# Axial attention: the second score product over all 128 rows, with the keys' low part stacked twice

## The chip, the cores and the metric

The kernel runs as one program on one core of a Trainium2 chip. The metric is the device time of that core in microseconds (us), the median of three runs. TensorE (PE) multiplies, VectorE (DVE), ScalarE (ACT) and GpSimd (POOL) do the elementwise work, and SyncE's queue (SP) issues nearly all transfers.

## The reference

Two layers of a transformer block work on 256 latent tokens and 256 context tokens of width 1024. In each layer three mixers (A: grouped-query attention with axial rotary embedding; B: gated linear attention; C: neighbourhood attention) read one projection of the normalised tokens, are merged under gates and projected out; then a mixture of 32 experts with two experts per token follows. Mixer A, cut to what matters:

```python
q = apply_rope(rms_norm(q_lat.reshape(B, L, 8, 64), q_norm), cos, sin)
k = apply_rope(rms_norm(k_lat.reshape(B, L, 2, 64), k_norm), cos, sin)
k_c = rms_norm(k_ctx.reshape(B, Lc, 2, 64), k_norm)
s = einsum('bqkgd,bskd->bkgqs', q, concat([k_c, k])) * 64 ** -0.5
o = einsum('bkgqs,bskd->bqkgd', softmax(s), v)
```

Eight query heads of 64 columns share two key heads. Latents attend to all 512 tokens. In layer 0 the context attends to its own 256 tokens as well; in layer 1 only the latents are computed on.

## The kernel before, in words

All large products are made in two parts: an operand is split into a high part that TensorE's fast fp32 form (fp32r) holds exactly, and a low rest. A full product is three matmuls, high by high, low by high and high by low (`mm3`, L380 to L382); the low-by-low term is left out. `split` (L291, L292) makes the two parts of the weights on ScalarE and VectorE from pieces of [128, 1024] that stream in (L373).

`attention` (mixer A) first projects keys and values (`projM`). For each of four token tiles `norm_rope` normalises and rotates the keys, and a staging tile `kst` [128 tokens, 2 key heads, 256 columns] is filled: the high part on ScalarE (L852) in columns 0 to 63, a copy of it on GpSimd (L853) in columns 64 to 127, the low part on VectorE (L854) in columns 128 to 191. Columns 192 to 255 are not used. TensorE transposes columns 0 to 127 into `kTs` (L859), so that the high part stands on rows 0 to 63 and again on rows 64 to 127, and columns 128 to 191 into rows 0 to 63 of `kTl` (L860); L861 and L862 copy both out of PSUM. Then the queries are projected, and `prep` makes for each tile `qT`: a head's query with its high part on rows 0 to 63 and its low part on rows 64 to 127 (transposes L880, copy L881).

A score tile of 128 queries is then made by two matmuls into one PSUM bank (`scores`): L888 multiplies all 128 rows of `qT` with `kTs` (high by high plus low by high), L889 multiplies rows 0 to 63 of `qT` with `kTl` (high by low) and adds to it. The page prints the used rows and columns of the array as `128*128` for the first and `64*128` for the second. For the latents these matmuls are 512 columns wide, for the context 256 columns.

`attend` runs over units (pairs of heads) and is one step ahead with the scores: `start` issues the scores of the next step, `finish` then makes the softmax of the step before (row maximum L796 on VectorE, exponential L799 on ScalarE, reciprocal L800 and scaling L802 on VectorE), the transposes of the probabilities (L944 for the latents, L950 for the context), their copies out of PSUM (L945, L951), the products with the values (L958, 64 columns of the array) and their split (L787, L788). A step of the latents issues L888, L889, L888, L889, a step of the context that sequence twice. Layer 0 has 8 steps of latents and 4 of context, layer 1 has 8 of latents.

Scores, transposes and value products share four PSUM banks; projections and merges have four others. The order on every engine is not written by hand: a planner takes the traced program, with priorities that follow the order of tracing, simulates all engines and their waits, and fixes each engine's order ahead of time. It puts matmuls of the merge of mixer B (`br`, `pT`) and of the projections of mixer C (`pM`) between the steps of the attention. Behind the mixers `out_norm` (matmuls `wo`) makes the tokens of the experts. The experts' weights (L1463, L1468) go into the place that the mixers' tiles leave, so those transfers wait for `wo` and later matmuls.

Of the kernel before, what the change touches and what calls it, by code (L numbers as in the profile page):

```python
# [27 lines left out]
# columns of w_in  # L28
A_Q, A_K, B_Q, B_K, B_V, B_R, B_A, C_Q, C_K, C_V, GATE = 0, 512, 768, 1024, 1280, 1792, 2304, 2336, 2848, 3360, 3872

# the order in which the mixers' weights stream in, one [128, 1024] piece each
# [27 lines left out]
# columns of the per-partition biases  # L59
# [9 lines left out]
# sections of the constants  # L69
# [9 lines left out]
# ranks of the experts of layer 0, by load but for experts 0 and 1, whose weights come in early:  # L79
# with 128 slots, with 64, the others with 32; the order of their halves of 128 slots  # L80
# [29 lines left out]
def groups(l):  # L110
    """The experts (in layer 0 by rank of their load) that share 256 slots, in two halves of one, two or four experts"""
    if l:
        return [((4 * d, 4 * d + 1), (4 * d + 2, 4 * d + 3)) for d in range(8)]
    a, b = 2 + NHOT, 2 + NHOT + NMID
    kinds = {"H": [(i,) for i in range(2, a)], "M": [(0, 1)] + [(i, i + 1) for i in range(a, b, 2)],
             "Q": [tuple(range(i, i + 4)) for i in range(b, NE, 4)]}
    halves = [kinds[k].pop(0) for k in HALVES]
    assert not any(kinds.values())
    return list(zip(halves[::2], halves[1::2]))


def _constants():
# [5 lines left out]
    i = np.arange(128)  # L128
# [4 lines left out]
    t = np.arange(256)  # L133
# [4 lines left out]
    cos, sin = np.cos(ang), np.sin(ang)  # L138
# [4 lines left out]
    # slots of the experts by rank  # L143
# [15 lines left out]
    # pairs of tokens of a block of 64 whose highest different bit is the level's  # L159
# [5 lines left out]
def _layout(inp):  # L165
    """The arrays of setup_inputs() as the program reads them."""
    g = {k: np.asarray(v) for k, v in inp.items()}
    f32 = np.float32
    o = {}
# [3 lines left out]
    # w_mod: [layer, group of four 512-column chunks, k tile, half of the group][partition][2 chunks x 512]  # L173
# [10 lines left out]
    # branches in the order in which they are merged: gla, attention, neighbourhood  # L184
# [42 lines left out]
    # the relative bias of every (query, key), outside of the window a constant; context keys have none  # L227
# [12 lines left out]
    # experts: [layer, expert][partition][six pieces of 2048]  # L240
# [9 lines left out]
class _Prog:  # L250
# [3 lines left out]
    # ---- tiles  # L254
# [14 lines left out]
    def rsqrt(self, v, w, tmp=None):  # L269
        """v ** -0.5 by Newton's method"""  # L270
# [18 lines left out]
    def split(self, src, hi, lo, eng=None):  # L289
        """hi + lo = src, exactly, each with 12 significant bits"""  # L290
        self.nc.scalar.copy(hi, src)  # L291
        (eng or self.nc.vector).tensor_tensor(lo, src, hi.bitcast(F32), op=ALU.subtract)  # L292

    def stats(self, x):
        """mean and 1 / sqrt(var + eps) of x [128, 1024]"""
# [9 lines left out]
    def norm0(self, x, xh, total=None):  # L305
        """xh = layer_norm0(x), both [128, 1024]; with the sums of x, ScalarE makes those of its squares"""
# [15 lines left out]
    def stats_all(self, xs, apart=False):  # L322
        """stats of tiles together: columns of means, of 1 / sqrt(var + eps), and of the opposites of their products"""
# [25 lines left out]
    def norm_quick(self, x, out, g, b):  # L349
        """out = layer_norm0(x) * g + b, on VectorE alone, and the sums of its rows; x is overwritten"""  # L350
        STT = self.nc.vector.scalar_tensor_tensor
        mu, r, _ = self.stats(x)
        s = self.small(2)
        STT(x, x, mu, g, op0=ALU.subtract, op1=ALU.mult)
        STT(out, x, r, b, op0=ALU.mult, op1=ALU.add, accum_out=s[:, 0:1])
        return s[:, 0:1]

    def norm(self, x, out, g, b, last=None):
        """layer_norm0(x) * g + b, in two steps"""
# [4 lines left out]
    # ---- streams of weights  # L364
    def raw(self, l):
        """A place for weights as they come in; the first ones of layer 1 can't wait for the tokens that use the others"""
# [17 lines left out]
    def projT(self, l, n, ntok):  # L384
        """[128 columns of w_in, tokens] = w^T h^T"""
# [7 lines left out]
    def projM(self, l, names, kper, width, tiles, sub=None):  # L393
        """[tokens, columns of w_in] for the token tiles, one bank each"""
# [17 lines left out]
    # ---- constants  # L412
# [42 lines left out]
    def open(self, name, side, tags):  # L455
        """A pool that shares its place with the one that follows it on the same side"""
# [7 lines left out]
    def later(self, n=400):  # L464
        """What is traced here gives way to the next n instructions"""
# [4 lines left out]
    # ---- modulation  # L470
    def modulation(self, l, groups, tag="raw", tag2="b2", ps="mod"):
        """[128, 512] of group g: row 32 j + s holds 512-column chunk 4 g + j for the latents (s = 0) and the context (s = 1)"""
# [11 lines left out]
        for g in groups:  # L484
# [19 lines left out]
            # the columns: [partition, scale or shift, stream, k tile]  # L504
# [18 lines left out]
    def mod_row(self, l, q, s, tag="o4"):  # L523
        """A modulation vector on every partition: [128, 1024]"""
# [7 lines left out]
    def norm_T(self, l, xs):  # L532
        """h^T of the mixers: modulated layer_norm0 of the four token tiles, in two parts"""
# [25 lines left out]
    # ---- per-layer vectors  # L559
    def vectors(self, l):  # L560
# [5 lines left out]
        # q and k norms with the rotary tables: [tile][q, k][cos, sin][64]  # L566
# [28 lines left out]
    # ---- branch B: gated linear attention  # L595
    def gla_gates(self, l):
        """log decays [tokens, (pair, direction, 2 x 64)] times 16, in two parts"""
# [14 lines left out]
    def gla_decay(self, pair):  # L612
        """Sums of the log decays (times 16) of each tile of tokens: up to and with a token (forward), up to a token (backward)"""
# [22 lines left out]
    def gla_pair(self, l, pair, T):  # L636
# [22 lines left out]
        # decays from a tile's start or end, of the queries and of the keys, in both directions  # L659
# [15 lines left out]
        # what a tile adds to the states of both directions  # L675
# [17 lines left out]
        # scores of a tile with itself, in blocks of 64: one level of the decay's tree after the other  # L693
# [47 lines left out]
        # the states before each tile  # L741
# [36 lines left out]
    # ---- the branches' outputs, transposed: tile k of branch i, in two parts  # L778
# [11 lines left out]
    # ---- attention  # L790
    def softmax(self, P, s, nh, w, mx=None, scale=1.0):
        """P [128, nh, w] = softmax over the last axis of scale * s"""
# [11 lines left out]
    def split2(self, src, hi, lo):  # L804
        """like split, from PSUM"""
# [3 lines left out]
    def norm_rope(self, l, z, nh, i, t):  # L809
        """rms_norm and rotary embedding of z [128, nh * 64] (i: 0 for q, 1 for k)"""  # L810
# [26 lines left out]
    def attention(self, l, T):  # L837
# [7 lines left out]
        for t in range(4):  # L845
# [8 lines left out]
            nc.vector.tensor_tensor(st[:, :, 128:192], o, hi, op=ALU.subtract)  # L854
            kst.append(st)
        for kv in range(2):
            p0, p1 = self.ps("kTs"), self.ps("kTl")
            for t in range(4):
                nc.tensor.transpose(p0[:, 128 * t:128 * t + 128], kst[t][:, kv, 0:128], self.ident)  # L859
                nc.tensor.transpose(p1[:64, 128 * t:128 * t + 128], kst[t][:, kv, 128:192], self.ident)  # L860
            nc.scalar.copy(kTs[:, kv], p0)  # L861
            nc.vector.tensor_copy(kTl[:64, kv], p1[:64])  # L862
# [21 lines left out]
        def scores(qT, kv, pair):  # L884
            def emit(o, i, ks):
                for h in range(2):
                    q = qT[i][:, 2 * pair + h]
                    mm(o[h], q, kTs[:, kv, ks], start=True, stop=False)  # L888
                    mm(o[h], q[:64], kTl[:64, kv, ks], start=False, stop=True)  # L889
# [12 lines left out]
    def attend(self, units):  # L902
        """softmax(scores) V of pairs of heads, for the latents over all keys or for the context over its own; one step ahead with the scores"""
# [64 lines left out]
        for n, (u, i) in enumerate(steps):  # L968
            o = start(u, i)
            # what the next units need is made before this one's end  # L970
# [52 lines left out]
    # ---- merge of the branches  # L1023
# [28 lines left out]
    def out_norm(self, l, T, src):  # L1052
        """x = layer_norm(alpha x + g1 (y w_out)), h2 = modulated layer_norm0(x)"""
# [64 lines left out]
    def h2_done(self, l, t):  # L1118
        """h2, in two parts"""
# [16 lines left out]
    def logits(self, l, t, h):  # L1136
        """the router's products of token tile t, from its layer_norm0"""
# [24 lines left out]
    def warm(self, n, x, name="warm"):  # L1162
        """Products that nothing reads, from x [128, some columns] on: they keep TensorE's clock up until its next work"""
# [6 lines left out]
    # ---- routing  # L1170
    def top2(self, l, t0, t1, T):
        """The two experts of the tokens of tiles t0 to t1, and their gates"""
        nc, c = self.nc, self.c
        TT, TS, STT, RED = nc.vector.tensor_tensor, nc.vector.tensor_scalar, nc.vector.scalar_tensor_tensor, nc.vector.tensor_reduce
        if t0 == 0:
# [6 lines left out]
            # the second choices' gates in two parts, what the first ones' are more in three  # L1182
# [18 lines left out]
        def mark(oh, x, m, weights, w, op=ALU.is_equal):  # L1201
            """op(1 where the maximum m comes first)"""
# [41 lines left out]
    def route(self, l, T):  # L1244
        """each token's place in its experts' slots"""
# [19 lines left out]
        # how many tokens before this one chose each expert, and how many chose it at all  # L1265
# [6 lines left out]
        if l == 0:  # L1272
            # experts by how many tokens chose them, on the partitions and along the rows
# [21 lines left out]
        # places beyond the slots' end, and below it  # L1295
# [17 lines left out]
        with self.later():  # L1313
            # what does not fit: blocks of 128 slots, expert after expert
# [9 lines left out]
            # from a token's place to its place there; negative where it fits  # L1324
# [7 lines left out]
            # the blocks' experts  # L1332
# [7 lines left out]
    def slot_rows(self, s, T):  # L1340
        """slots of all tokens on every partition, first and second choices"""
# [12 lines left out]
    # ---- experts  # L1354
    def one_hot(self, iota, w, T, d):
        """[tokens, slots]: 1 where the token has the slot, and where it is the first choice's"""
# [7 lines left out]
    def slot_gates(self, p, OH, O1, T):  # L1364
        """p [slots, 5]: the parts of the gates of the slots' tokens"""
# [6 lines left out]
    def gather_T(self, OH, w, T):  # L1372
        """the slots' tokens, transposed: [d, k, slot]"""
# [14 lines left out]
    def spots(self, rows, col, T):  # L1388
        """[slots, tokens]: 1 where the token has the slot"""
# [8 lines left out]
    def expert_tail(self, h1, h3, gate, w2, halves, end=False):  # L1398
        """Y = (silu(h1) * h3 * gate) w2, in two parts; w2(f, n, i): weights of half i"""
# [19 lines left out]
    def combine(self, CY, T, last):  # L1419
        """x += g2 * the experts' outputs"""  # L1420
# [13 lines left out]
    def expert(self, l, u):  # L1434
        """The weights of an expert (in layer 0 of rank u): [128, six pieces, 2048]"""
# [7 lines left out]
    def load(self, l, us, n, js, step=2048, most=99, after=None):  # L1443
        """Pieces js of the weights of the experts us"""
# [3 lines left out]
        for j in js:  # L1448
            for i in range(len(us)):
# [7 lines left out]
                if n < 6 or n >= 6 + extra:  # L1457
                    x = self.t([128, 2048], "pre" if n < 0 else "ew" if n < 6 else "ewb", name="ew")
                    if after is not None:
                        # not before other weights  # L1460
# [10 lines left out]
    def experts(self, l, T):  # L1471
# [51 lines left out]
        # the second products of one pair of experts come after the first ones of the next  # L1523
# [10 lines left out]
    def overflow(self, l, T):  # L1534
        """the tokens beyond an expert's slots, in blocks of 128"""
# [44 lines left out]
    def final_norm(self, l, T, lgb):  # L1580
        """x = layer_norm(alpha x + g2 experts)"""
# [32 lines left out]
    def run(self):  # L1614
# [7 lines left out]
        for l in range(NL):  # L1622
# [42 lines left out]
            if l:  # L1665
                # what the context's tokens leave
# [44 lines left out]
```

## Time and profile before

| what | value |
|---|---|
| time, median of 3 runs | 2171.39 us (2170.97 to 2172.95) |
| profiled execution, span | 2169.8 us |
| median beyond that span | 1.6 us |
| PE busy | 1989.3 us, 92% of the span |
| DVE busy | 968.1 us, 45% |
| ACT busy | 561.9 us, 26% |
| POOL busy | 272.2 us, 13% |
| DMA | 562.41 MB, mean 259 GB/s |

The span is the profiled execution from its first to its last instruction. Busy shares are means over stages with different limits: in the mixers (about 200 to 650 us and 1240 to 1650 us) little is transferred, while in the experts (about 650 to 1207 us and 1647 to 2150 us) the DMA engines are busy nearly all the time. Matmuls overlap in PE's pipeline, so the time that one matmul takes from the stream is the distance of its start to the next start, not its duration.

### The profile page before, as it was taken

The numbers are of one execution on the slowest core, as the hardware profiler recorded it, in microseconds if no ns is written. First come the engines' busy times: TensorE is split into PE (matmuls) and PEld (weight loads), VectorE is DVE, ScalarE is ACT, GpSimd is POOL, SyncE is SP. The second block draws the span as 40 slices with busy tenths as digits, with TensorE's granted clock in tenths as the row PEclk, the third lists the DMA queues.
The fourth block names the chain that finished last, engine by engine and source line by source line (L and its number), as shares of the span: only waits on it lengthen the run. The fifth ranks groups of instructions, "written<-read, shape, count | busy, mean of one in ns | idle before, by whom it ended". The sixth has DMA issues, their size and how long they took to land. (4 is left out here: it accounts for less than half of the span.)

```text
span 2169.8 us, 28061 instructions
## 1 busy us (share of the span) xinstructions
PE 1989.3 (92%) x10749; PEld 1179.2 (54%) x10749; DVE 968.1 (45%) x2236; ACT 561.9 (26%) x992; POOL 272.2 (13%) x260
## 2 busy tenths in 40 slices
PE   5999999999998898989899598999996999999995
PEld 2676766777885353445253165786795433333321
DVE  4676765564388131222022765766648222221213
ACT  3443334343333000000000254444543111010000
POOL 1322100011110010111011222100020000000000
PEclk9999999999999999999999798999997999999998
DMA  7436212223328899999998723632466999999995
GB/s 289 164 121 218 78 59 69 93 83 96 126 79 334 367 420 421 371 385 421 419 369 370 270 85 112 197 118 74 139 207 250 387 421 423 421 423 422 421 422 222
DMA packets 113987, 562.41 MB, mean 259 GB/s; under 512 B 13302, under 2 KB 14838, under 8 KB 72120
## 3 DMA queue, kind: packets, MB, share of 16 engines
q1 hardware_dynamic: 113272, 558.85, 66.9%
q8 instruction: 87, 1.43, 0.3%
q10 hardware_dynamic: 576, 1.70, 0.2%
q14 instruction: 52, 0.43, 0.1%
HBM read 557.36 MB, written 3.15 MB: 258 GB/s over the span
## 5 line engine op out<-in xcount | busy, mean ns | idle before, releaser
L1506 PE MATMUL h<-ew,XT 128*64 128x512 f32 (+2 forms) x2048 | 478.3, 611 | 40.0 <-DMA ew<-in_ew_dram 39.8
L1506 PEld LDWEIGHTS h<-ew,XT 128*64 128x64 f32 (+2 forms) x2048 | 146.6, 135 | 326.3 <-issue 248.8
L1414 PE MATMUL Y<-ew,aT 128*64 128x512 f32 (+2 forms) x1024 | 252.4, 598 | 10.1 <-DMA ew<-in_ew_dram 7.9
L292 DVE TENSOR_TENSOR wlo<-raw,whi 128x1024 fp32r<-128x1024 f32 (+1 forms) x140 | 178.9, 1278 | 139.6 <-ACT whi L291 138.4
L1432 POOL TENSOR_TENSOR x<-x,ct 128x512 f32<-128x512 f32 x82 | 105.0, 1307 | 1003.5 <-DVE ct L1431 879.8
L380 PE MATMUL pT<-hThi,whi 128*128 128x512 f32 (+1 forms) x576 | 202.9, 352 | 1.5 <-ACT whi L291 0.8
L291 ACT CAST whi<-raw 128x1024 fp32r<-128x1024 f32 (+1 forms) x140 | 145.4, 1039 | 226.5 <-PE pT L381 116.2
L382 PE MATMUL pT<-hThi,wlo 128*128 128x512 f32 (+1 forms) x576 | 202.3, 351 | 0.2 <-DVE wlo L292 0.2
L381 PE MATMUL pT<-hTlo,whi 128*128 128x512 f32 (+1 forms) x576 | 202.1, 351 | 0.0
L1403 DVE SCALAR_TENSOR_TENSOR act<-h,s,sl 128x512 f32<-128x512 f32 x30 | 22.5, 751 | 325.4 <-PE h L1506 270.5
L1414 PEld LDWEIGHTS Y<-ew,aT 128*64 128x64 f32 (+2 forms) x1024 | 76.0, 133 | 151.0 <-issue 125.7
L807 DVE TENSOR_TENSOR Yl<-Y,Yh 128x512 fp32r<-128x512 f32 x60 | 41.4, 690 | 257.2 <-ACT Yh L806 254.1
L806 ACT CAST Yh<-Y 128x512 fp32r<-128x512 f32 x60 | 35.2, 587 | 462.5 <-PE Y L1414 462.5
L380 PEld LDWEIGHTS pT<-hThi,whi 128*128 128x128 f32 x576 | 109.5, 190 | 22.4 <-issue 4.1
L382 PEld LDWEIGHTS pT<-hThi,wlo 128*128 128x128 f32 x576 | 109.5, 190 | 16.2 <-issue 2.9
L381 PEld LDWEIGHTS pT<-hTlo,whi 128*128 128x128 f32 x576 | 109.6, 190 | 15.2 <-issue 3.0
L380 PE MATMUL pM<-whi,hThi 128*128 128x512 f32 (+1 forms) x304 | 110.7, 370 | 3.6 <-ACT qTkT L645 1.9
L381 PE MATMUL pM<-wlo,hThi 128*128 128x512 f32 (+1 forms) x304 | 111.8, 369 | 0.0
L382 PE MATMUL pM<-whi,hTlo 128*128 128x512 f32 (+1 forms) x304 | 111.7, 368 | 0.0
L495 PE MATMUL mod<-wmod,sT 128*32 128x512 f32 x320 | 75.0, 624 | 23.4 <-DVE s L343 14.8
L1407 ACT COPY aT<-aT 128x512 f32<-128x512 f32 x30 | 17.6, 586 | 292.7 <-PE aT L1406 292.7
L1383 PE MATMUL XT<-OH,h2hi 128*128 128x256 f32 x352 | 89.1, 290 | 0.0
(363 smaller groups left out, 3093.4 us busy)
## 6 DMA issues: line engine op xcount, KB each, us to landing
ew<-in_ew_dram SPq DMA_DIRECT2D x326, 1024.0 KB, 13.8
raw<-in_w_dram SPq DMA_DIRECT2D x145, 512.0 KB, 3.7
ew<-in_ew_dram SPq DMA_DIRECT2D x116, 512.0 KB, 13.5
wmod<-in_wmod_dram SPq DMA_DIRECT2D x96, 512.0 KB, 6.1
nb<-in_nb_dram SPq DMA_DIRECT2D x32, 256.0 KB, 3.8
g<-md SPq DMA_DIRECT2D x12, 256.0 KB, 7.6
row<-in_ln_dram SPq DMA_DIRECT2D x4, 512.0 KB, 4.9
lgb<-in_ln_dram SPq DMA_DIRECT2D x4, 512.0 KB, 12.0
```

Source lines behind the costliest of these rows:

```text
L291: self.nc.scalar.copy(hi, src)
L292: (eng or self.nc.vector).tensor_tensor(lo, src, hi.bitcast(F32), op=ALU.subtract)
L380: mm(out, lh, rh, start=start, stop=False)
L381: mm(out, lh, rl, start=False, stop=False)
L382: mm(out, ll, rh, start=False, stop=stop)
L495: nc.tensor.matmul(p[32 * j:32 * j + 32, :], self.sT[:, k, :], raws[j // 2][:, 512 * (j % 2):512 * (j % 2) + 512], start=k == 0, stop=k == 7)
L806: self.nc.scalar.copy(hi, src)
L807: self.nc.vector.tensor_tensor(lo, src, hi.bitcast(F32), op=ALU.subtract)
L1383: mm(p[:, w * j:w * j + w], self.h2s[t][part][:, 128 * k:128 * k + 128], OH[:, t], start=t == 0 and part == 0, stop=t == T - 1 and part == 1)
L1414: mm(y[m * i:m * i + m, :], aT[:, 128 * f + m * i:128 * f + m * i + m], w2(f, n, i), start=f == 0, stop=f == 3)
L1432: (nc.vector if last and n else nc.gpsimd).tensor_tensor(self.x1[t][:, ns], self.x1[t][:, ns], tmp, op=ALU.add)
L1506: mm(h[m * i:m * i + m, :], XTs[dp][:, k, 128 * pr + m * i:128 * pr + m * i + m], w[i, 2 * q + k // 4][k % 4], start=k == 0, stop=k == 7)
```

## The change

The staging tile's unused columns get a copy of the keys' low part (a new GpSimd instruction per token tile, 8 in all). The transposes of the low part take 128 columns in place of 64, the copy out of PSUM takes all 128 rows, and the second score product multiplies all 128 rows of `qT` with `kTl`. It thereby adds the low-by-low term that was left out. The number of matmuls, transposes and PSUM copies stays as it was. The diff also strips comments and docstrings, which moves line numbers and nothing else.

```diff
             nc.vector.tensor_tensor(st[:, :, 128:192], o, hi, op=ALU.subtract)
+            nc.gpsimd.tensor_copy(st[:, :, 192:256], st[:, :, 128:192])
             kst.append(st)
...
-                nc.tensor.transpose(p1[:64, 128 * t:128 * t + 128], kst[t][:, kv, 128:192], self.ident)
+                nc.tensor.transpose(p1[:, 128 * t:128 * t + 128], kst[t][:, kv, 128:256], self.ident)
             nc.scalar.copy(kTs[:, kv], p0)
-            nc.vector.tensor_copy(kTl[:64, kv], p1[:64])
+            nc.vector.tensor_copy(kTl[:, kv], p1)
...
                     mm(o[h], q, kTs[:, kv, ks], start=True, stop=False)
-                    mm(o[h], q[:64], kTl[:64, kv, ks], start=False, stop=True)
+                    mm(o[h], q, kTl[:, kv, ks], start=False, stop=True)
```

## Rows read from the trace of the kernel before

**Rows 1.** Busy time of each engine by stretch; last columns: granted clock, DMA share, GB/s.
```profile
262.00:376.00 114.00, 113.97 (x536) 80.39 (x534) 63.92 (x137) 47.86 (x101) 2.56 (x2) 1.00 0.21 61
392.00:650.00 258.00, 257.95 (x1213) 197.49 (x1212) 142.65 (x268) 92.85 (x158) 28.44 (x19) 1.00 0.31 99
650.00:1220.00 570.00, 508.09 (x2604) 237.95 (x2604) 167.69 (x427) 62.37 (x108) 66.65 (x53) 0.96 0.93 377
1405.00:1484.00 79.00, 77.77 (x464) 60.55 (x464) 55.84 (x113) 36.40 (x67) 3.06 (x3) 1.00 0.33 101
1484.00:1646.00 162.00, 158.59 (x1056) 135.01 (x1055) 95.36 (x160) 72.88 (x118) 20.84 (x20) 0.99 0.49 152
```
**Rows 2.** Instructions of the tile kTl: durations in ns, first and last start, forms.
```profile
L889 PE MATMUL S<-kTl,qTA x48: 379/492/502, 263.8 to 1483.1; 64*128 64x512 f32 x32, 64*128 64x256 f32 x16
...
L860 PE MATMUL kTl<-cst,kst x16: 270/271/273, 221.5 to 1407.7; 128*64 128x128 f32 x16
L862 DVE CAST kTl<-kTl x4: 673/678/683, 236.3 to 1409.1; 64x512 fp32r<-64x512 f32 x4
```
**Rows 3.** The same view of the tile kTs, its transposes.
```profile
L859 PE MATMUL kTs<-cst,kst x16: 270/272/273, 221.4 to 1406.9; 128*128 128x128 f32 x16
```
**Rows 4.** PE in order of time, a latent step in layer 0: start, duration, instruction.
```profile
266.16 0.40 PE L380 MATMUL pT<-hThi,whi 128*128 128x512 f32 x1
...
268.89 0.40 PE L888 MATMUL S<-kTs,qTA 128*128 128x512 f32 x1
269.22 0.50 PE L889 MATMUL S<-kTl,qTA 64*128 64x512 f32 x1
269.65 0.50 PE L888 MATMUL S<-kTs,qTA 128*128 128x512 f32 x1
270.08 0.50 PE L889 MATMUL S<-kTl,qTA 64*128 64x512 f32 x1
270.51 0.50 PE L380 MATMUL pT<-hThi,whi 128*128 128x512 f32 x1
270.85 0.39 PE L381 MATMUL pT<-hTlo,whi 128*128 128x512 f32 x1
```
**Rows 5.** PE's weight loads in order of time, the same stretch; in brackets idle time before.
```profile
266.17 0.19 PEld L381 LDWEIGHTS pT<-hTlo,whi 128*128 128x128 f32 x1
...
270.08 0.18 PEld L889 LDWEIGHTS S<-kTl,qTA 64*128 64x128 f32 x1 [0.25 <-issue]
```
**Rows 6.** PE in order of time, a context step in layer 0, first score and next transposes.
```profile
343.28 0.28 PE L888 MATMUL S<-kTs,qTA 128*128 128x256 f32 x1
...
345.68 1.09 PE L944 MATMUL PT<-cst,P 128*128 128x128 f32 x8
```
**Rows 7.** PE in order of time, both ends of 23 intervals of 256 columns, layer 1.
```profile
1400.01 0.28 PE L381 MATMUL pT<-hTlo,whi 128*128 128x256 f32 x1
...
1402.75 0.28 PE L380 MATMUL br<-o,whi 128*128 128x256 f32 x1
```
**Rows 8.** Instructions of the tile kst on GpSimd, columns as in rows 2.
```profile
L853 POOL COPY kst<-kst x8: 418/420/1155, 216.7 to 1404.5; 128x128 f32<-128x128 f32 x8
```
**Rows 9.** GpSimd in order of time, what follows layer 0's last staging copy.
```profile
246.63 1.29 POOL L828 TENSOR_TENSOR rope<-sq,rope 128x512 f32<-128x512 f32 x1 [14.78 <-DVE sq L822]
```
**Rows 10.** PE in order of time, attention of layer 1: its first score and late waits.
```profile
1441.56 0.48 PE L888 MATMUL S<-kTs,qTA 128*128 128x512 f32 x1
...
1462.95 0.50 PE L888 MATMUL S<-kTs,qTA 128*128 128x512 f32 x1
...
1467.88 0.50 PE L888 MATMUL S<-kTs,qTA 128*128 128x512 f32 x1 [0.24 <-ACT PT L945]
...
1469.59 0.66 PE L944 MATMUL PT<-cst,P 128*128 128x128 f32 x4
...
1486.78 0.63 PE L944 MATMUL PT<-cst,P 128*128 128x128 f32 x4 [2.19 <-DVE P L802]
```
**Rows 11.** VectorE in order of time, scaling of the probabilities that these transposes read.
```profile
1469.45 0.48 DVE L802 TENSOR_SCALAR P<-P,s 128x512 f32<-128x512 f32 x1
```
**Rows 12.** Waits of SP's queue: us in total, times, longest.
```profile
SPq L493 <- PE wo L381: 34.2, 1, 34.2
```

## The prediction

> **What bounds the kernel now.** I read the busy times by stretch first, since the page's shares mix stages. In the stretch that holds layer 0's attention of mixer A, PE is busy 113.97 of 114 us while VectorE has 63.92 and the DMA engines 0.21 of it; in the rest of those mixers PE has 257.95 of 258. Layer 1's attention has 77.77 of 79, the mixers behind it 158.59 of 162 [rows 1]. The reader is to see that PE alone sets the pace there, at a granted clock of 1.00 (0.99 in the last), its level of 2.4 GHz. In layer 0's experts the DMA share is 0.93, but their transfers begin when the mixers' last matmuls free the place: SP's queue stands 34.2 us in one wait for `wo` [rows 12]. So what PE saves in the mixers moves the experts forward by as much, and the DMA-bound stage keeps its length.
>
> Then I read PE in order of time and took distances between starts. A run of 128-row matmuls, 512 columns wide, goes from 266.16 to 268.89 in 12 intervals: 2.73 / 12 = 0.2275 us each. Then the scores come: L888 to L889 0.33, L889 to L888 0.43, 0.43, L889 to the following L380 0.43, and L380 still takes 0.34 [rows 4]. A 64-row matmul between 128-row ones thus costs about 0.1 us before and 0.1 behind each of its two borders. The weight loads show how: in the run a load starts with the matmul before its own (266.17 against 266.16), at a border only with its own matmul, after 0.25 us idle (270.08 against 270.08) [rows 4, 5].
>
> **The change, part by part.**
>
> Second score product, 512 columns: 32 matmuls [rows 2], in 16 steps of two pairs. One step occupies 268.89 to 270.85, five intervals, 1.96 us [rows 4]. With all five at the run's distance it would be 5 x 0.2275 = 1.14. Saved: 0.82 per step, 16 x 0.82 = 13.1 us, half of it (6.6) in each layer. The changed L888 and L889 have the form of `mm3`'s matmuls in that run: 128 rows and columns, fp32r, one bank for consecutive ones, the same weights loaded twice in succession. That is why I price them by it. The other end is no gain, 0.
>
> Second score product, 256 columns: 16 matmuls [rows 2], in four steps of four pairs, all in layer 0. One step goes from 343.28 to 345.68, eight intervals, 2.40 us [rows 6]. The nearest 128-row run of that width has 23 intervals in 2.74 us, 0.119 each [rows 7]; 8 x 0.119 = 0.95. Saved: 1.45 per step, 5.8 us in all.
>
> Sum on PE: 13.1 + 5.8 = 18.9 us, 12.4 in layer 0 and 6.5 in layer 1.
>
> Now what isn't kept. In layer 0 PE has other work at hand throughout, so nearly all is kept. In layer 1 PE runs out of filler near the end: five of its eight steps (5 x 0.82 = 4.1 us) lie at 1462.95 and behind it [rows 10]. There PE waits 0.24 us at a time for copies out of PSUM, and 2.19 us for the last probabilities [rows 10]. One step is plainly tied to the softmax: the scaling ends at 1469.93 (1469.45 + 0.48) while the first of its transposes start at 1469.59 [rows 10, 11]; shortening the scores before them only makes PE wait, and I write off 0.8. Another 0.3 I take off for a second step with little room, and 0.9 (an estimate, about a sixth of what these and the last context step save, 4.1 + 1.45) for steps that stand next to the 64-column value products, whose own border stays. Sum kept: 18.9 - 2.0 = 16.9 us. The bounds: all 18.9; or nothing from the five late steps and the last context step, 18.9 - 5.6 = 13.3.
>
> GpSimd's new copies: 8 of the form of L853, which takes 0.42 us in the median and 1.16 at most [rows 8]. Each waits for the low part on VectorE, so the transposes of the low part come 0.5 to 1.5 us later. Cover: the last copy of `kTl` starts at 236.3 in layer 0 and 1409.1 in layer 1 [rows 2], the first scores stand by 263.8 and 1441.56 [rows 2, 10], 27 and 32 us later, with projections of the queries on PE between. Behind the copy on GpSimd stands the rotation of the queries, after 14.78 us of idle time [rows 9], or for earlier tiles the next tile's value copy and rotation, whose consumer is again a covered `kst`. I take 0; without the cover it would be up to 4 x 1.5 = 6 us a layer. Below nothing it cannot be: it is added work.
>
> Transposes of the low part: 16, from 64 to 128 columns of the array, which is the form of L859: 272 ns against 271 [rows 2, 3]. I take 0, between -0.1 and +0.5 us. L862 over 128 rows in place of 64 has the same 512 columns; four of them, at 0.68 us each, under the same cover: 0.
>
> Profiled span 2169.8 - 16.9 = 2152.9. The median lies 1.6 us above that span, so I predict 2154.5.
>
> One rule speaks against this. The Trainium skill ("TensorE: Matmul & The Clock Gate", Part 3, "What overlaps and what doesn't") says that a weight load runs beside a matmul in flight only when the two use different row groups. By it full-height matmuls would never overlap their loads and the change would give nothing; the trace disagrees, since the 128-row load at 266.17 runs beside the 128-row matmul of 266.16 [rows 4, 5]. That would be the second rival below.
>
> **The rivals.**
>
> The softmax takes over. If VectorE and ScalarE set the pace of the steps, a shorter score only makes PE idle. For it: the late waits of layer 1 [rows 10, 11]. Against it: VectorE has 63.92 of 114 us in layer 0, and PE fills every gap with merges and projections [rows 1]. It would keep perhaps half, 9.4 us: 2162.
>
> The gap stays. The 0.43 us could come from something that the change leaves, such as loading the same queries twice in succession or adding to the bank just written. Then the change is only added copies under cover: 2171 to 2172. Against it: L380 and L381 in the run load the same weights and add to the same bank at 0.2275 [rows 4], and the border costs as much on an unrelated L380 behind the scores.
>
> Slower: the planner draws a new order from the first changed instruction on, and it may put a transfer with a long wait ahead of experts' weights in SP's queue. The place is the change from mixers to experts. The price is that of the one long wait of this kind, 34.2 us [rows 12], because a DMA share of 0.93 [rows 1] leaves no room to make up lost queue time: 2154.5 + 34.2 = 2188.7. It decides as soon as more than 16.9 us of queue time are lost. Against it: a few instructions of 0.42 us and some modelled durations are all that the planner sees changed. The same redrawing can also come out better; I know no row for its size.
>
> **How the numbers follow.** Forecast (13.3 to 18.9 us kept, 2152.5 to 2158): 0.74. Softmax takes over: 0.11. Gap stays: 0.06. Slower order: 0.05. A luckier order, better than 2152.5: 0.04. About 0.2%, 4.3 us, is what a measurement of this kernel can tell from no change; faster by more than that is 0.74 + 0.11 + 0.04 = 0.89, of which I give 0.02 to no change, since between forecast and nothing kept there is all that lies between. Faster 0.87, same 0.08, slower 0.05. The range reaches up to the softmax case with a little more for a redrawn order, 2164, and down to 2149, 18.9 us kept plus 3.5 for a better order.
>
> **What would show it.** The changed second product should print 128*128 and follow the first at 0.23 us (0.12 for 256 columns), with its weight load starting beside the matmul before. A latent step's five intervals should make 1.14 us, a context step's eight 0.95. The experts of layer 0 should start about 12 us earlier and the last instruction about 17. The late waits of layer 1 should grow by about 1 us. I am wrong if the distances stay at 0.43, if PE's idle time in the attention grows by as much as the scores shrink, or if the experts don't move with the mixers.

## The result and the profile after

The changed kernel takes 2148.64 us (median of 4 runs, 2147.55 to 2150.77) against 2171.18 us of the kernel before (4 runs, 2167.34 to 2172.95): 22.5 us less, a ratio of 0.9894 with an interval of 0.9876 to 0.9912. The sign is as forecast, and so is the mechanism of the product; the size is 5.6 us more than the 16.9 forecast, and the time lies 0.4 us below the range's lower end of 2149. The profiled execution spans 2148.9 us, 20.9 less than that of before. The medians of the runs below leave out two executions in a slow state, 2559.50 us in e7 and 10758.42 us in e10.

The page's first line of busy times: PE has 16.3 us less (1989.3 before), GpSimd 5.3 more for the eight copies.

```profile
PE 1973.0 (92%) x10749; PEld 1179.0 (55%) x10749; DVE 964.7 (45%) x2236; ACT 561.5 (26%) x992; POOL 277.5 (13%) x268
```

The tile `kTl` in the changed kernel (columns as in [rows 2]; from L855 on its lines stand one lower, so L889 of before is L890):

```profile
L890 PE MATMUL S<-kTl,qTA x48: 281/392/398, 265.3 to 1462.7; 128*128 128x512 f32 x32, 128*128 128x256 f32 x16
L861 PE MATMUL kTl<-cst,kst x16: 270/272/330, 222.5 to 1392.8; 128*128 128x128 f32 x16
L863 DVE CAST kTl<-kTl x4: 681/686/691, 238.0 to 1394.2; 128x512 fp32r<-128x512 f32 x4
```

All 48 second products now use 128 rows, and their median falls from 492 to 392 ns. The wider transposes cost what the narrow ones did (272 against 271 ns [rows 2]). The new copy, in the view of the tile `kst`, is shorter than the form by which I priced it (292 ns in the median against 420 [rows 8]):

```profile
L855 POOL COPY kst<-kst x8: 288/292/1378, 218.0 to 1389.9; 128x128 f32<-128x128 f32 x8
```

PE in order of time (start, duration, instruction, in brackets idle time before and its releaser): a latent step, a context step's ends, a transpose between mixers and experts, and the late wait of layer 1.

```profile
269.48 0.39 PE L382 MATMUL pT<-hThi,wlo 128*128 128x512 f32 x1
269.70 0.39 PE L889 MATMUL S<-kTs,qTA 128*128 128x512 f32 x1
269.93 0.40 PE L890 MATMUL S<-kTl,qTA 128*128 128x512 f32 x1
270.17 0.39 PE L889 MATMUL S<-kTs,qTA 128*128 128x512 f32 x1
270.40 0.39 PE L890 MATMUL S<-kTl,qTA 128*128 128x512 f32 x1
270.62 0.39 PE L380 MATMUL pT<-hThi,whi 128*128 128x512 f32 x1
270.85 0.39 PE L381 MATMUL pT<-hTlo,whi 128*128 128x512 f32 x1
...
338.73 0.28 PE L889 MATMUL S<-kTs,qTA 128*128 128x256 f32 x1
...
339.69 1.04 PE L945 MATMUL PT<-cst,P 128*128 128x128 f32 x8
...
661.08 1.09 PE L1151 MATMUL h2T<-cst,h 128*128 128x128 f32 x8
...
1466.19 0.81 PE L945 MATMUL PT<-cst,P 128*128 128x128 f32 x4 [2.19 <-DVE P L802]
```

The five intervals from 269.70 to 270.85 take 1.15 us (1.96 before [rows 4]; forecast 1.14), the context step from 338.73 to 339.69 takes 0.96 (2.40 before [rows 6]; forecast 0.95). The weight loads, in order of time, show the same thing from the other side:

```profile
269.71 0.19 PEld L890 LDWEIGHTS S<-kTl,qTA 128*128 128x128 f32 x1
...
270.40 0.19 PEld L380 LDWEIGHTS pT<-hThi,whi 128*128 128x128 f32 x1
```

L890's load starts at 269.71, with the L889 ahead of it (269.70) and 0.22 us ahead of its own matmul (269.93). Before, it started with its own matmul [rows 5].

The Trainium skill's rule ("TensorE: Matmul & The Clock Gate", Part 3, "What overlaps and what doesn't"), that a weight load overlaps a matmul in flight only where the row groups differ, does not hold for these full-height pairs.

Busy time by stretch (bounds; length, then PE, PEld, DVE, ACT, POOL busy; last three columns granted clock, DMA share, GB/s). The first two lines answer to [rows 1]. From the third on, the bounds are the issue times of the same transfers in SP's queue, so that stretches of different kernels can be compared: attention of layer 0, the passage from mixers to experts (it holds the first six issues of experts' weights), the experts of layer 0, attention of layer 1, its tail.

```profile
251.00:365.00 114.00, 114.00 (x593) 89.46 (x592) 72.51 (x157) 52.13 (x108) 4.71 (x3) 1.00 0.23 66
381.00:639.40 258.40, 258.32 (x1214) 197.74 (x1213) 142.44 (x268) 92.67 (x158) 28.50 (x20) 1.00 0.32 100
231.28:366.49 135.21, 133.51 (x683) 105.12 (x682) 87.69 (x186) 59.63 (x122) 8.53 (x6) 1.00 0.26 78
639.41:673.50 34.09, 31.49 (x202) 17.70 (x201) 26.07 (x112) 17.20 (x32) 0.00 (x0) 1.00 0.97 380
673.50:1194.07 520.57, 472.80 (x2397) 219.89 (x2396) 131.94 (x276) 42.16 (x73) 66.05 (x52) 0.97 0.93 379
1389.61:1464.07 74.46, 72.97 (x466) 60.97 (x466) 54.83 (x113) 36.71 (x68) 3.17 (x4) 1.00 0.36 107
1464.07:1487.33 23.26, 20.75 (x109) 16.27 (x109) 11.18 (x18) 6.88 (x13) 2.74 (x2) 0.85 0.22 68
```

The same stretches of the kernel before:

```profile
230.37:376.99 146.62, 145.63 (x682) 106.06 (x681) 88.14 (x186) 59.88 (x122) 7.14 (x5) 1.00 0.24 73
649.72:684.78 35.06, 31.89 (x202) 17.64 (x201) 26.01 (x111) 17.33 (x32) 0.00 (x0) 1.00 0.98 385
684.78:1207.38 522.60, 474.16 (x2397) 220.13 (x2396) 131.97 (x277) 42.20 (x73) 66.10 (x52) 0.97 0.92 377
1405.21:1484.66 79.45, 78.34 (x466) 60.90 (x466) 55.67 (x113) 36.66 (x68) 2.85 (x3) 1.00 0.33 100
1484.66:1506.82 22.16, 19.47 (x109) 15.43 (x109) 11.18 (x18) 6.88 (x13) 2.75 (x2) 0.92 0.23 71
```

The reader is to see two things. The attention is shorter by 11.41 and 4.99 us, and PE stays nearly as full as it was. But some time also went where no score of mixer A is computed: 0.97 us in the passage and 2.03 in the experts of layer 0. The experiments ask where that comes from.

### The profile page after: what moved, and what is told of

Its sections match the earlier page's. It is cut to its first block, busy times and chain, and to the rows that moved or that the text cites. A ratio compares the mean times of both kernels' runs of the same rounds, so it can differ in the third digit from the quotient of the medians.

```text
span 2148.9 us, 28075 instructions
## 1 busy us (share of the span) xinstructions
PE 1973.0 (92%) x10749; PEld 1179.0 (55%) x10749; DVE 964.7 (45%) x2236; ACT 561.5 (26%) x992; POOL 277.5 (13%) x268
## 3 DMA queue, kind: packets, MB, share of 16 engines
q8 instruction: 87, 1.43, 0.3%
## 5 line engine op out<-in xcount | busy, mean ns | idle before, releaser
L1415 PE MATMUL Y<-ew,aT 128*64 128x512 f32 (+2 forms) x1024 | 250.4, 598 | 10.2 <-DMA ew<-in_ew_dram 7.8
L1404 DVE SCALAR_TENSOR_TENSOR act<-h,s,sl 128x512 f32<-128x512 f32 x30 | 22.5, 751 | 317.6 <-PE h L1507 263.9
L495 PE MATMUL mod<-wmod,sT 128*32 128x512 f32 x320 | 75.2, 636 | 22.5 <-DVE s L341 14.1
```

Of the source, the lines that this page charges most:

```text
L495: nc.tensor.matmul(p[32 * j:32 * j + 32, :], self.sT[:, k, :], raws[j // 2][:, 512 * (j % 2):512 * (j % 2) + 512], start=k == 0, stop=k == 7)
L1415: mm(y[m * i:m * i + m, :], aT[:, 128 * f + m * i:128 * f + m * i + m], w2(f, n, i), start=f == 0, stop=f == 3)
```

## The experiments

The theory: the product without borders earns what was forecast, and the rest comes from the order of instructions that the planner drew anew. Rivals: the product was priced too low, or the rest is scatter between executions.

The planner's orders of before and after differ on PE at some 80 spots, from the key transposes on: among them the `logit` and `mod` matmuls behind the mixers of layer 0, some in its experts, and mixer B of layer 1. SP's order is the same.

**Only the copies and the order (e1).** The 64-row product put back into the changed kernel; all else stays, and the order on every engine is that of the changed kernel.

```diff
-                    mm(o[h], q, kTl[:, kv, ks], start=False, stop=True)
+                    mm(o[h], q[:64], kTl[:64, kv, ks], start=False, stop=True)
```

> The changed kernel with its second score product back on 64 rows; the copies and the 128-column transposes stay, and every engine's order is that of the changed kernel, instruction by instruction. Left out again: the low-by-low term. Theory A (the product is worth about what its borders add up to, 15 to 17 us, and the other 5 to 6 us of the 22.5 come from the order that the planner drew anew): about 5 us faster than before, 2166. Rival B (the saving on the product was priced too low, and order and copies give nothing): the time of before, 2171. Rival C (the surplus is what one execution differs from another): near 2171 with a spread of several us.

Measured: 2167.67 us against 2171.72, ratio 0.9982 [0.9966, 0.9997]; by the ratio 3.9 us less (0.7 to 7.4) without any change in the product. The same five stretches:

```profile
227.75:374.81 147.06, 145.36 (x682) 105.99 (x681) 88.10 (x186) 59.75 (x121) 8.51 (x6) 1.00 0.24 72
647.73:681.82 34.09, 31.48 (x202) 17.70 (x201) 26.07 (x112) 17.21 (x32) 0.00 (x0) 1.00 0.97 384
681.82:1202.67 520.85, 471.33 (x2397) 220.03 (x2396) 131.99 (x276) 42.20 (x73) 66.03 (x52) 0.97 0.93 379
1398.23:1477.77 79.54, 78.42 (x466) 60.96 (x466) 55.08 (x113) 36.85 (x68) 3.18 (x4) 1.00 0.32 100
1477.77:1500.63 22.86, 20.62 (x109) 16.09 (x109) 11.25 (x18) 6.89 (x13) 2.73 (x2) 0.85 0.22 70
```

Attention is as long as before (147.06 and 79.54), while the passage and the experts are as short as after (34.09 and 520.85). What the product itself earns is the difference of two kernels of one order, after less e1: 147.06 - 135.21 = 11.85 in layer 0 and 79.54 - 74.46 = 5.08 in layer 1, together 16.93 us.

**Only the product (e2, repeated as e10).** The kernel before with 128 rows, transposes of columns 64 to 191, no copies. Its scores leave out high by low and count high by high twice, so they are other numbers; the instructions on every engine are as many as before. Its order is that of before but for the key transposes (10 spots).

```diff
-                nc.tensor.transpose(p1[:64, 128 * t:128 * t + 128], kst[t][:, kv, 128:192], self.ident)
+                nc.tensor.transpose(p1[:, 128 * t:128 * t + 128], kst[t][:, kv, 64:192], self.ident)
```

> The kernel before with the second score product over 128 rows and no copies: the transposes take columns 64 to 191 of the staging tile, so rows 0 to 63 of the second operand hold the keys' high part and rows 64 to 127 the low part; the scores are therefore other numbers, the work of each instruction is that of the changed kernel without the copies. Every engine's order is that of the kernel before but for the place of a few key transposes. Theory A: the product alone, 15 to 17 us faster than before, 2154 to 2156. Rival B: 22 us faster, 2149. The copies on GpSimd, if they cost anything, would make it faster than the changed kernel by up to 6 us; I expect 0.

Measured: 2153.05 us, ratio 0.9903 [0.9882, 0.9923]. By the ratio that is 16.7 to 25.6 us less, so the time by itself does not exclude that the product was priced too low; the stretches say more.

```profile
230.24:364.78 134.54, 133.54 (x683) 105.16 (x682) 87.68 (x186) 59.57 (x122) 7.14 (x5) 1.00 0.25 78
637.36:672.43 35.07, 31.90 (x202) 17.65 (x201) 26.01 (x111) 17.31 (x32) 0.00 (x0) 1.00 0.99 386
672.43:1196.20 523.77, 474.24 (x2397) 220.56 (x2396) 132.09 (x277) 42.16 (x73) 66.03 (x52) 0.97 0.92 376
1392.48:1466.83 74.35, 72.87 (x466) 61.06 (x466) 55.35 (x113) 36.50 (x68) 2.88 (x3) 1.00 0.34 107
1466.83:1487.49 20.66, 17.96 (x109) 14.17 (x109) 11.18 (x18) 6.88 (x13) 2.73 (x2) 1.00 0.25 77
```

The mirror image: attention shorter by 12.08 and 5.10 us, the passage at 35.07 and the experts at 523.77, as long as before or longer. So, by the stretches of attention, the product is worth 16.9 to 17.2 us in either order.

The three kernels against the kernel before, by stretch of the profiled executions (us):

| stretch | after | e1: order, no product | e2: product, no new order |
|---|---|---|---|
| ahead of the attention of layer 0 | +0.9 | -2.6 | -0.1 |
| attention, layer 0 | -11.4 | +0.4 | -12.1 |
| other mixers, layer 0 | +0.2 | +0.2 | -0.2 |
| passage to the experts | -0.97 | -0.97 | 0.0 |
| experts, layer 0 | -2.0 | -1.8 | +1.2 |
| up to the attention of layer 1 | -2.3 | -2.3 | -1.6 |
| attention, layer 1 | -5.0 | +0.1 | -5.1 |
| its tail (1484.66 to 1506.82 before) | +1.1 | +0.7 | -1.5 |
| from there to the end | -1.4 | -0.8 | +0.8 |
| span | -20.9 | -7.0 | -18.5 |

Outside the attention, and without the stretch ahead of it, that is -5.4 for after, -5.0 for e1 and -1.3 for e2. But such a sum scatters: the kernels after and before, executed again, gave -5.2 (e4), -0.3 (e9) and +0.6 (e5). What goes with the order has to be looked for in shorter stretches, and there are two in which it stands clear of scatter.

One is the end of the experts of layer 0, from the issue of the last five of their weights to the end of the stretch. It takes 33.71 to 33.73 us in the six executions with the new order there (after, e1, e4, e6, e9, e11) and 35.07 to 35.11 in the seven others, so the order is worth 1.4 us. Before, then after, SP and PE in order of time:

```profile
1172.28 4.30 SPq L1463 DMA_DIRECT2D ew<-in_ew_dram  x5
1182.69 9.78 PE L1414 MATMUL Y<-ew,aT 128*64 128x512 f32 x38
1192.40 1.20 PE L1428 MATMUL cb<-Yh,C 128*128 128x512 f32 x4
...
1160.36 4.30 SPq L1464 DMA_DIRECT2D ew<-in_ew_dram  x5
1170.76 8.06 PE L1415 MATMUL Y<-ew,aT 128*64 128x512 f32 x34
1179.43 1.20 PE L1429 MATMUL cb<-Yh,C 128*128 128x512 f32 x4 [0.62 <-ACT Yh L806]
```

In the new order four of the experts' products (`Y`) stand behind the `cb` matmuls in place of ahead of them, and counted from the issue of the weights `cb` comes 1.05 us earlier (19.07 us against 20.12). The rest of the experts' stretch differs between executions of one order by up to 3.6 us (486.0 to 489.6 us in the new one).

The other is the passage, with 0.97 us, and there most of the cause can be seen. In the kernel before, PE comes to the transposes of the token norm too early (one line of PE in order of time):

```profile
672.29 1.09 PE L1150 MATMUL h2T<-cst,h 128*128 128x128 f32 x8 [0.58 <-ACT h L320]
```

In the new order more `mod` matmuls stand ahead of that transpose, and it has no wait (661.08, in the lines of PE after). That is 0.58 of the 0.97 us; for the other 0.4 PE is busy less with the same 202 matmuls (31.89 and 31.49 us), for a reason that was not looked for.

**Grouping the 64-row products (e3).** The kernel before, with both first products of a pair of heads and then both second ones, to price the border by itself.

```diff
-                    mm(o[h], q[:64], kTl[:64, kv, ks], start=False, stop=True)
+                for h in range(2):
+                    mm(o[h], qT[i][:64, 2 * pair + h], kTl[:64, kv, ks], start=False, stop=True)
```

> The kernel before with a step's score products in another sequence, the two 128-row ones first and then the two 64-row ones, all on the rows they had. If the cost sits at the borders between 128-row and 64-row products (0.2 us each, half before and half behind), a latent step has two borders in place of four and saves 0.41 us (16 steps, 6.6 us), a context step four in place of eight and saves about 0.75 (4 steps, 3.0): 9.6 us faster, 2161.5, and the second of two 64-row products in a row follows the first at 0.33 us. Rival D (a 64-row product is slow by itself, wherever it stands): distances of 0.43 stay and the time is that of before, 2171. The planner's order differs in the attention of layer 0, which may add or take a few us.

Measured: 2168.96 us, ratio 0.9982 [0.9967, 0.9997]. The gain of 9.6 us did not come, since the planner put most steps back into the alternating order; only 4 of the 20 stayed grouped (5 of 24 pairs). One of these, PE in order of time:

```profile
263.39 0.71 PE L887 MATMUL S<-kTs,qTA 128*128 128x512 f32 x2
264.03 0.73 PE L889 MATMUL S<-kTl,qTA 64*128 64x512 f32 x2
264.69 0.50 PE L381 MATMUL pT<-hTlo,whi 128*128 128x512 f32 x1
```

Two 64-row products in a row take 264.69 - 264.03 = 0.66 us, against 2 x 0.43 = 0.86 alternating [rows 4]. The other two grouped pairs of that width take 0.66 us as well. So a 64-row product is not slow by itself: one border fewer is worth 0.2 us where it happens. The total says nothing on the price.

**The changed kernel and the kernel before again (e4, e5).** No edit; they measure the scatter.

> The changed kernel again, in the same session as the three others. Theory A and B: 2148 to 2150 again. Rival C: the gain over before shrinks towards 17 us, 2154.

> The kernel before once more, for a second profile. Theory A (the surplus lies in the order): stretch by stretch it agrees with the first profile within about 1 us behind 180 us; from the first modulation load behind layer 0's mixers to the first load of the final norm (649.72 to 1207.38 in the first profile, 557.7 us) again 557 to 559. Rival C (executions differ by as much as the surplus): the same stretch comes out 3 us shorter or longer, and the stretch from 1253.88 to 1405.21 (151.3 us) by 2.5.

Measured: 2151.98 us, ratio 0.9902 [0.9880, 0.9924], and one execution of before, 2168.63. In e4 the passage is again 34.09 us, the experts of layer 0 520.48 and the attention of layer 1 74.45; in e5 they are 35.08, 522.24 and 79.45. The stretch ahead of the change is 3.1 us shorter in e4 than in after and 3.4 shorter in e5 than in before, so a few us of a span are scatter. The passage and the attention repeat to 0.2 us; the experts do not always (below).

**One layer at a time (e6, e7).** The change behind a condition on the layer.

```diff
+        R = 128 if l == 0 else 64
...
+                    mm(o[h], q[:R], kTl[:R, kv, ks], start=False, stop=True)
```

> The change in layer 0 alone; layer 1 has the 64-row product without copies. The order is that of the changed kernel up to the key transposes of layer 1. Theory A: 11.4 us off in layer 0's attention, about 3 off in layer 0's experts and 2.5 off in layer 1 ahead of its attention through the order, nothing in layer 1's attention: 17 us faster, 2154. Rival B or C (no worth in the order): 12 us faster, 2159.

> The change in layer 1 alone. The order is that of the kernel before up to layer 1's key transposes. Theory A: no difference before 1400 us, then 4 to 6.6 us off in layer 1's attention and up to 1 in its experts: 2165 to 2167. Rival B or C: the same in the attention; a difference of some us before 1400, where all instructions and their order are those of before, would speak for rival C.

Measured: layer 0 alone 2154.33 us, ratio 0.9923 [0.9900, 0.9946]; layer 1 alone 2164.02, ratio 0.9966 [0.9951, 0.9982]. Layer 0 alone has the new order up to the transposes of layer 1, and with it the passage of 34.09 us and experts of 519.73; its attention falls from 146.62 to 135.23. Layer 1 alone keeps the order of before up to there, with 35.07 and 524.83; its attention falls from 79.45 to 74.44. So the passage shortens where the new order is, not where the product is. The experts' 524.83, in an order that is that of before, are 2.2 us longer than before: their whole length scatters by as much as the difference looked for.

**The copy without GpSimd (e8, e11).** In e8 one VectorE subtraction writes the low part to both places, which gives a third order; in e11 a second subtraction does, with the order of after up to the key transposes of layer 1.

```diff
-            nc.gpsimd.tensor_copy(st[:, :, 192:256], st[:, :, 128:192])
+            nc.vector.tensor_tensor(st[:, :, 192:256], o, hi, op=ALU.subtract)
```

> The changed kernel without the copies on GpSimd: one VectorE instruction writes the keys' low part into both places, 256 columns in place of 128 (about 0.15 us longer, 8 times, under the same cover). All scores as in the changed kernel. The planner's order is a third one: as before up to layer 0's experts, own in their second half and in layer 1. Theory A: 12 us off in layer 0's attention and 5 to 6.6 in layer 1's, and whatever the third order gives or takes in between, a few us either way: 2149 to 2157. Rival B: the 22 us of the changed kernel again, 2149. The copies' own cost: 0.

> The changed kernel once more, beside the next two on the same chip. Both theories: 2148 to 2153 us, ratio 0.988 to 0.992 against the kernel before. If the new order of the planner is worth what the kernel with only the copies and the order showed (3.9 us, interval 0.7 to 7.4), this kernel stands 2 to 5 us below the one without copies; if that difference was scatter of executions, the two agree within 1 us and the product alone is worth more than I priced it at (about 19 to 20 us in place of 16.9).

> The 128-row second product without GpSimd's copies, in the order of the kernel before; the low part of the keys stands on rows 64 to 127 only, so the high-by-low term is left out. Theory that the order earns the surplus: 2152 to 2156 us, the stretch between mixers and experts of layer 0 (650 to 685 us) unchanged at 35.06 us and the experts of layer 0 at the length of before. Rival that the surplus is the product or scatter: the same time as the changed kernel, within 1 us.

> The second place of the low part is written by another VectorE subtract in place of the copy on GpSimd; the order is that of the changed kernel but for some transposes of the keys and few others. If the order earns the surplus: within 2 us of the changed kernel, with the 0.97 us less between mixers and experts (34.09 in place of 35.06). If GpSimd's copies themselves did something (a delay that happens to help), it stands 2 us or more above the changed kernel.

Measured: e8 2152.84 us, ratio 0.9913 [0.9889, 0.9937], with a passage of 35.08. On one chip: after (e9) 2148.91, ratio 0.9884 [0.9862, 0.9906]; without copies (e10) 2152.81, 0.9904 [0.9882, 0.9925]; copy on VectorE (e11) 2151.95, 0.9905 [0.9885, 0.9925].

```profile
638.96:673.05 34.09, 31.48 (x202) 17.70 (x201) 26.06 (x112) 17.21 (x32) 0.00 (x0) 1.00 0.97 381
```

e11 has no new copy on GpSimd and yet the shorter passage (the line above), in the order that it shares; its profiled span is 2149.5. The experts of layer 0 take 523.28 us in e9, in the new order, as long as in the order of before; only their end and the passage (34.09) are as short as in after. The median of e11 stands 3.0 us above e9, more than the 2 that the theory allowed, but the intervals overlap, so the times decide nothing between them. The gap between after and the kernel without copies was 1.1 us in the first comparison (2151.98 and 2153.05) and 3.9 in the second, where 2 to 5 were expected of the order. None of the variants is faster than the changed kernel.

## Why the prediction was right, and where it was wrong

**The mechanism and its size.** "Saved: 0.82 per step" and "1.45 per step" came out at 0.81 and 1.44. "Sum kept: 18.9 - 2.0 = 16.9 us": 16.93 in the order of after, 17.18 in that of before. Some 0.5 us were lost in layer 0 and 1.4 in layer 1. The late waits of layer 1 grew by 0.7 us where the order is the same, a little less than the 1 us that I named: PE's waits for the probabilities are 2.2 us in e1 and 2.9 after. Against before (2.8 us from 1405.21 to 1506.82) no growth shows. The write-offs of 0.8, 0.3 and 0.9 were never measured apart; that their sum is right to 0.1 is in part luck.

**What moved with it.** The experts of layer 0 follow the mixers: the first issue of their weights behind `wo` comes at 656.45 us in place of 666.64, 10.2 earlier, and the first behind the passage at 673.50 in place of 684.78, 11.3 earlier (forecast about 12). That "the DMA-bound stage keeps its length" holds for the product alone, within what executions of one kernel scatter there. SP's wait for `wo` is as long as before (34.2 [rows 12]):

```profile
SPq L493 <- PE wo L381: 34.1, 1, 34.1
```

**The step that failed** is the price of GpSimd's copies: "I take 0 ... Below nothing it cannot be: it is added work." As work they cost next to nothing, as priced: 5.3 us more on GpSimd, under cover. But they are also input to the planner, and the sum has no term for the order that it draws. e1 and e2 show that it is the copies, not the wider transposes or the taller product, that made it draw a new order, and that this order runs some 4 us faster (3.9, 0.7 to 7.4, timed). Of these, 0.97 us in the passage and 1.4 at the end of layer 0's experts are seen in every execution with that order and in no other. I had this case, "a luckier order", and gave it 0.04 and 3.5 us below the bound of 18.9 kept, while I spent 0.05 and a price of 34 us on the slower one. With 16.9 for the product and 4 for the order the sum is 2171.4 - 20.9 = 2150.5, inside the range. The rest, up to the 22.5 measured, is within the scatter: of the changed kernel's three medians, 2148.64, 2151.98 and 2148.91, the second lies inside the range too. That the first lies 0.4 us below it is within the scatter too; that it lies 5.9 us below 2154.5 is for the most part the order.

**The rivals.** Softmax takes over: no, PE is busy 114.00 of 114 us in layer 0 and 72.97 of 74.46 in layer 1. The gap stays: no. A slower order with a long wait for SP: no, SP's order is unchanged. The rival of the experiments that the product was priced too low falls with 16.93 and 17.18, by stretches; the times of e2 and e10 alone would not decide it. Scatter explains the passage's 0.97 us in no way, since it is 34.09 in every execution with the new order and 35.06 to 35.08 in every other; it does explain several microseconds elsewhere, in the experts above all.

**What stays open.** The passage is traced to a wait, and the end of layer 0's experts to moved matmuls, each for the larger part; no run moved these instructions alone. The stretch from there up to the attention of layer 1 (197.83 us before) takes 195.2 to 195.7 us in the five executions in the order of after (after, e1, e4, e6, e9) and 196.2 to 198.7 in the others, so the order gains there too, but since the others scatter by 2.5 us, how much cannot be said.

## What to carry to other kernels

Where a run of full-height matmuls is broken by half-height ones, count the borders and price each from the distances of starts; the full-height product is then worth more than the rows it wastes. Where a planner fixes the order, every added instruction, however well hidden, is a new draw for the whole program: give that draw a range of its own on both sides (here some 4 us, 0.2%), and measure it by putting back the old operand in the new order. Where whole stretches scatter by as much, compare short pieces of them over all executions of either order.

## What the runs showed of the hardware

TensorE's clock makes part of the scatter. In the tail of layer 1's attention PE waits 2.19 us for the last probabilities, before and after alike. The changed kernel in stretches of 4 us:

```profile
1464.00:1468.00 4.00, 1.43 (x8) 1.09 (x8) 3.25 (x8) 2.23 (x6) 0.00 (x0) 0.81 0.42 131
1468.00:1472.00 4.00, 4.00 (x17) 2.91 (x16) 2.23 (x4) 0.00 (x0) 0.00 (x0) 0.50 0.02 4
1472.00:1476.00 4.00, 4.00 (x27) 3.26 (x28) 1.20 (x2) 1.35 (x2) 0.37 (x1) 0.83 0.00 0
```

And the kernel without copies (e2):

```profile
1466.00:1470.00 4.00, 1.39 (x11) 0.94 (x9) 2.71 (x8) 2.43 (x6) 0.00 (x0) 1.00 0.44 131
1470.00:1474.00 4.00, 3.85 (x28) 3.33 (x29) 3.00 (x6) 0.20 (x1) 0.00 (x0) 1.00 0.00 1
```

After nearly the same idle time (1.43 and 1.39 us busy of 4) the granted clock falls to 0.50, the level of 1.2 GHz, in the one and stays at 1.00 in the other, and the tail takes 23.26 or 20.66 us. That is the tail's +1.1 and -1.5 in the table. Two executions of the kernel before, in one order, had 0.92 (22.16 us) and 0.85 (23.35 us, e5), so how long the low clock lasts isn't decided by the order alone. Whether it comes at all was the same in every execution of one kernel: 0.85, 0.85 and 0.86 in the three of the changed kernel (after, e4, e9), 1.00 in both without copies (e2, e10, 20.66 us each). What decides that is not shown.

The Trainium skill ("TensorE: Matmul & The Clock Gate", Part 1, "What's actually happening") says that the window over which the clock gate looks at activity runs free and is not reset when a kernel starts. The two executions of before agree, with 0.92 and 0.85 behind the same wait; that the same kernel's clock falls in one execution and not in another, no run here shows.
